# Scheduling the small matmuls of HGRN at top priority in a hybrid encoder trunk

## The chip, the cores and the metric

The kernel runs on one core of a Trainium2 chip. The metric is the device time of one execution in microseconds (us). The engines are named as in the profile: PE is the matmul engine (TensorE) and PEld its loading of weights, DVE the vector engine, ACT the scalar engine, POOL is GpSimd, and SP starts the transfers.

## The reference

The kernel computes a bidirectional encoder trunk: 2 layers, a sequence of 1024 positions, width 1024, float32. Every layer normalises its input, sends it through one projection with 8192 output columns, and lets three groups of heads work on slices of the result side by side: an mLSTM group (4 heads), an HGRN2 group (6 heads of 128 channels) and a differential attention group (4 heads). Each group's output is gated, and one output projection adds the sum to the layer's input. The change touches HGRN only:

```
def hgrn2_chunkwise(q, f, v):            # S_t = diag(f_t) S_{t-1} + (1 - f_t) i_t^T ; o_t = S_t^T q_t
    ...
    A = cumsum(log f)
    decay[t, s, c] = exp(A[t, c] - A[s, c])  for s <= t
    scores = einsum("bhtc,bhtsc,bhsc->bhts", qb, decay, kb)      # kb = 1 - f
    o = scores @ v + (q * exp(A)) @ S_state
    ...
def hgrn2_bidirectional(q, f_fwd, f_bwd, v):
    fwd = hgrn2_chunkwise(q, f_fwd, v)
    bwd = flip(hgrn2_chunkwise(flip(q), flip(f_bwd), flip(v)))
    return fwd + bwd
```

The score of a pair of positions thus weighs each channel by the product of all forget gates between the two.

## The kernel before, in words

**Stages of a layer.** First come the norm and the transposition of the input, then the xm projection with convolution and gates, then two long parts that overlap: the mLSTM recurrence (lines 575 to 663: 4 heads, 8 chunks of 128 positions in each direction; per step the products num, L633 to L638, and the state products st, L648 and L649; per head the products q, L593, and qk, L602), and HGRN with the rest of the projections. Then follow attention with its own projections (aqk, avz), and the output projection (op, L1066).

**Projections.** `proj_channel` (L295) and `proj_token` (L308) multiply the input by blocks of the weight. Each product is split in three matmuls of the type fp32r (high by high, high by low, low by high), with 512 columns streamed in `proj_channel` (tiles pc_...) and 256 or 384 in `proj_token` (tiles pt_...). Their PSUM tiles come from a pair with the tag pj.

**HGRN of one head** (`hgrn_rest`, L684). The query q and the two sets of gates are projected (hq, hff, hfb). Then the scores are built for the 8 chunks of 128 positions at once, by a hierarchy of levels in place of the sum of logarithms. The diagonal (tile dg, L718) is a product of the summed keys kd with q. Level lv (0 to 6) handles pairs of positions that lie in neighbouring blocks of 2^lv positions. For the levels 0 to 4 ACT copies a mixed set of keys to kt (L736), and 16 matmuls (8 chunks by 2 halves, L742) multiply 64 by 64 blocks over 128 channels. DVE then takes the entries of this level into sd by a masked copy (L723). Level 5 has 32 matmuls of 32 by 32, level 6 has 16 of 64 by 64 (L759 and L761), and both write to the PSUM tile that level 4 began. Between the levels DVE multiplies the keys ks (L780) and queries qp (L781) by the gates of the block, and halves the row of gate products (L785). So the levels of a head form a chain: kt and qp of the level, matmuls, then the update for the next. In the program's names all tiles of the levels are lv, those of the diagonal dg. They come from PSUM tiles of 1024 columns with the tag s2, two of them, which the later steps of the head use too: the transposed keys kst, the state products sb and sf, the output ho and its transposition hyT.

The matmuls of dg and lv take float32 operands and write to one half of the partitions, so the trace gives the tile as 128x64 (128x32 at level 5) and two records per matmul: 32 records for a group of 16 matmuls, 64 for level 5.

**What sets the order.** The kernel is written in program order and a scheduler puts it into one list per engine, beforehand, with a simulated timeline. It keeps an order of priority: an instruction's priority is its place in the program, and of those that are ready for an engine the earliest in the program goes first. A PSUM or SBUF slot is given to a tile when its first writer is scheduled. On the chip each engine works through its list. HGRN stands behind mLSTM in the program, and its heads are called in this order:

```
for step in "i0 r0 i1 r1 i2 r2 i3 r3 i4 r4 i5 o0 r5 z0 o1 z1".split():
    {"i": hgrn_iz, "r": hgrn_rest, "o": mlstm_om, "z": mlstm_zm}[step[0]](int(step[1]))
```

Here i is the projection of HGRN's values and gate (hiz, L681), r the rest of a head, o and z are the mLSTM group's gates (om, zm). The tiles qp, ks and T0 of a head have one buffer each, the values v and gates gt two.

Of the kernel before, what the change touches and what calls it, by code (L numbers as in the profile page):

```python
# [17 lines left out]
P = 128  # L18
D = 1024
S = 1024  # L20
NT = S // P
# [64 lines left out]
def raw(ap, off, dims):  # L86
    return bass.AP(ap.tensor, ap.offset + off, [list(ap.ap[0])] + [list(d) for d in dims])
# [3 lines left out]
def trunk(ctx, tc, x_in, positions, w_in, w_out, pvec, rvec, out, dbg=None):  # L91
    nc = tc.nc
# [10 lines left out]
    def ps_mx(name):  # L103
        return pp.tile([P, 512], F32, tag="mx", name=name)

    def ps_s2(name):
        return pp.tile([P, 1024], F32, tag="s2", name=name)
# [239 lines left out]
    for l in range(DEPTH):  # L347
# [14 lines left out]
        for half in range(2):  # L362
# [21 lines left out]
            for k in range(8):  # L384
                ps = ps_mx(f"hT{l}{half}{k}")
# [15 lines left out]
        with tc.tile_pool(name=f"ma{l}", bufs=2) as ma:  # L401
# [38 lines left out]
            for i in range(3):  # L440
                parts = load_win(l, ("xm", i)) if l or i else xm0
                for jj in range(2):
# [19 lines left out]
                    for src, rhs, dd, nm in ((xc, WA[j], xct_d, "a"), (xm, BV[j], v_d, "v")):  # L462
                        tk = ma.tile([P, NT, P], F32, tag="tk", name=f"tk{nm}{l}{j}", bufs=1)
                        for t0 in range(0, NT, 4):
                            ps = ps_s2(f"tk{nm}{l}{j}{t0}")
                            for t in range(4):
                                o = (t // 2) * 512 + (t % 2) * 144
# [27 lines left out]
        with tc.tile_pool(name=f"mb{l}", bufs=1) as mB:  # L495
# [27 lines left out]
            for d in range(2):  # L523
                rows = []
                for nm, src in (("i", igt), ("f", lgf)):
                    rt = mB.tile([4, S], F32, tag="gr" + nm, name=f"gr{nm}{l}{d}", bufs=2)
                    for half in range(2):
                        ps = ps_mx(f"gr{nm}{l}{d}{half}")
# [12 lines left out]
                for c in order:  # L541
                    sl = slice(c * P, (c + 1) * P)
# [10 lines left out]
                for i, (src, dst) in enumerate(((ir, a_tok), (br, b_tok), (mu, m_tok))):  # L553
                    ps = ps_mx(f"gt{l}{d}{i}")
# [17 lines left out]
        with tc.tile_pool(name=f"mc{l}", bufs=1) as mp:  # L572
            for hd in range(MH):
# [14 lines left out]
                q = mp.tile([P, 2, S], F32, tag="m8", name=f"q{l}{hd}", bufs=2)  # L588
                for i, g in enumerate((G[jA], G[jC][:, hh_])):
                    for half in range(2):  # L590
                        sl = slice(half * 512, (half + 1) * 512)
                        ps = ps_mx(f"q{l}{hd}{i}{half}")
# [3 lines left out]
                for half in range(2):  # L596
                    ps = ps_mx(f"qk{l}{hd}{half}")
                    for c4 in range(4):
                        c = half * 4 + c4
                        sl = slice(c * P, (c + 1) * P)  # L600
# [26 lines left out]
                for i in range(NT):  # L627
                    for d in range(2):
                        c = i if d == 0 else NT - 1 - i
                        C = Cs[d]  # L630
                        sl = slice(c * P, (c + 1) * P)
# [11 lines left out]
                        if i < NT - 1:  # L643
                            ks = kst[2 * d + i % 2]
# [22 lines left out]
        def slab(name, tag, bufs=None):  # L667
            return gp.tile([P, S], F32, tag=tag, name=f"{name}{l}", bufs=bufs or 1)
# [15 lines left out]
        def hgrn_rest(hd):  # L684
            v, gt = hvg[hd]
            T0 = gp.tile([P, 2, S], F32, tag="T0", name=f"T0_{l}{hd}")
            qp = gp.tile([P, 2, S], F32, tag="qp", name=f"qp_{l}{hd}")
            ks = gp.tile([P, 2, S], F32, tag="ks", name=f"ks_{l}{hd}")
            q = qp[:, 1]
# [20 lines left out]
            kd = slab(f"kd{hd}", "ha")  # L710
# [1 line left out]
            nc.vector.tensor_tensor(qp[:, 0], T0[:, 0], q, op=ALU.mult)  # L712
            sd = gp.tile([P, NT * 64], F32, tag="sc", name=f"sd{l}{hd}")
            ps = ps_s2(f"dg{l}{hd}")[:, :512]
            for c in range(NT):
                for g in range(2):
                    sl = slice(c * P + g * 64, c * P + g * 64 + 64)
                    nc.tensor.matmul(ps[g * 64:g * 64 + 64, c * 64:c * 64 + 64], kd[:, sl], q[:, sl], start=True, stop=True)  # L718
            nc.scalar.activation(sd, ps, AF.Copy)
            nc.vector.tensor_tensor(qp[:, 1], T0[:, 1], q, op=ALU.mult)  # L720

            def merge(ps, b):
                nc.vector.copy_predicated(sd.rearrange("p (c t) -> p c t", c=NT),  # L723
                                          lvl[b].unsqueeze(1).broadcast_to([P, NT, 64]),
                                          ps[:, :512].rearrange("p (c t) -> p c t", c=NT))
# [4 lines left out]
            pbase = None  # L730
            for lv in range(7):
                hs = 1 << lv
                if lv <= 4:
                    kt = slab(f"kt{hd}{lv}", "kt")
                    nb = S // (2 * hs)
                    nc.scalar.activation(raw(kt, 0, [[2 * hs, nb], [hs, 2], [1, hs]]),  # L736
                                         raw(ks, 0, [[2 * hs, nb], [hs + S, 2], [1, hs]]), AF.Copy)
                    ps = ps_s2(f"lv{l}{hd}{lv}")
                    for c in range(NT):
                        for g in range(2):  # L740
                            o = c * P + g * 64
                            nc.tensor.matmul(ps[g * 64:g * 64 + 64, c * 64:c * 64 + 64], kt[:, o:o + 64],  # L742
                                             raw(qp, o, [[2 * hs, 64 // (2 * hs)], [hs + S, 2], [1, hs]]),
                                             start=True, stop=True)
                    if lv < 4:
                        merge(ps, lv)
                    else:
                        pbase = ps
                else:
                    for c in range(NT):  # L750
                        for m in range(P // (2 * hs)):
                            f0 = 2 * hs * m
                            s0 = f0 + hs
                            b0 = c * P
                            if lv == 5:
                                o1, o2 = c * 64 + hs, c * 64
                            else:
                                o1 = o2 = 512 + c * 64
                            nc.tensor.matmul(pbase[f0:f0 + hs, o1:o1 + hs], ks[:, 0, b0 + f0:b0 + f0 + hs],  # L759
                                             qp[:, 1, b0 + s0:b0 + s0 + hs], start=True, stop=True, skip_group_check=True)  # L760
                            nc.tensor.matmul(pbase[s0:s0 + hs, o2:o2 + hs], ks[:, 1, b0 + s0:b0 + s0 + hs],  # L761
                                             qp[:, 0, b0 + f0:b0 + f0 + hs], start=True, stop=True, skip_group_check=True)
                    if lv == 5:
                        merge(pbase, 4)
                    else:
                        sc = slab(f"sc{hd}", "kt")
                        scv = sc.rearrange("p (c g t) -> p c g t", c=NT, g=2)
                        p6 = pbase[:, 512:].rearrange("p (c t) -> p c t", c=NT)
                        sdv = sd.rearrange("p (c t) -> p c t", c=NT)
                        for g in range(2):  # L770
                            gs = slice(g * 64, g * 64 + 64)
                            nc.scalar.activation(scv[gs, :, 1 - g], p6[gs], AF.Copy)
                            nc.vector.tensor_copy(scv[gs, :, g], sdv[gs])
                nb = S // (2 * hs)
                el = [[2 * hs, nb], [hs + S, 2], [1, hs]]
                tq = raw(T, 1, [[2, nb], [W - 1, 2], [0, hs]])
                tk = raw(T, W + 1, [[2, nb], [-W - 1, 2], [0, hs]])
                qv = raw(qp, 0, el)
                kv = raw(ks, 0, el)
                nc.vector.tensor_tensor(kv, kv, tk, op=ALU.mult)  # L780
                nc.vector.tensor_tensor(qv, qv, tq, op=ALU.mult)  # L781
                base = T1 if lv % 2 == 0 else T0
                a0 = raw(T, 0, [[W, 2], [2, W // 2]])
                a1 = raw(T, 1, [[W, 2], [2, W // 2]])
                nc.vector.tensor_tensor(raw(base, 0, [[W // 2, 2], [1, W // 2]]), a0, a1, op=ALU.mult)  # L785
                T = base
                W //= 2
# [4 lines left out]
            for w in (1, 0):  # L792
                ps = ps_s2(f"kst{l}{hd}{w}")
                for c in range(NT):
                    sl = slice(c * P, (c + 1) * P)
# [4 lines left out]
            for c in range(NT - 1, 0, -1):  # L800
                sl = slice(c * P, (c + 1) * P)
                nc.tensor.matmul(psb[:, sl], kst_t[:, 1, sl], v[:, c], start=True, stop=True)
            for c in range(NT - 1, 0, -1):
                sl = slice(c * P, (c + 1) * P)
# [6 lines left out]
            for c in range(NT - 1):  # L811
                sl = slice(c * P, (c + 1) * P)
                nc.tensor.matmul(psf[:, sl], kst_t[:, 0, sl], v[:, c], start=True, stop=True)
            Sf = ks[:, 0].rearrange("p (c v) -> p c v", c=NT)
            for c in range(NT - 1):
                sl = slice(c * P, (c + 1) * P)
# [7 lines left out]
            for c in range(NT):  # L824
                sl = slice(c * P, (c + 1) * P)
# [6 lines left out]
            for c in range(NT):  # L832
                sl = slice(c * P, (c + 1) * P)
                nc.scalar.activation(jk, po[:, sl], AF.Square, accum_out=ss[:, c:c + 1])
            rstd(ss, r, P)
            for c in range(NT):
                sl = slice(c * P, (c + 1) * P)
                nc.vector.scalar_tensor_tensor(gt[:, c], po[:, sl], r[:, c:c + 1], gt[:, c], op0=ALU.mult, op1=ALU.mult)
            ps = ps_s2(f"hyT{l}{hd}")
            for c in range(NT):  # L840
                sl = slice(c * P, (c + 1) * P)
# [59 lines left out]
        for step in "i0 r0 i1 r1 i2 r2 i3 r3 i4 r4 i5 o0 r5 z0 o1 z1".split():  # L901
            {"i": hgrn_iz, "r": hgrn_rest, "o": mlstm_om, "z": mlstm_zm}[step[0]](int(step[1]))
# [3 lines left out]
        with tc.tile_pool(name=f"at{l}", bufs=2) as ap, tc.tile_pool(name=f"aw{l}", bufs=1) as aw:  # L906
# [79 lines left out]
            for hd in range(AH):  # L986
# [5 lines left out]
                for qt in range(NT):  # L992
                    qs = slice(qt * P, (qt + 1) * P)
                    ex, ls = [], []
                    for n in range(2):
                        ps = ps_s2(f"S{l}{hd}{qt}{n}")
# [20 lines left out]
                    for kb in range(2):  # L1017
                        ps = ps_mx(f"wT{l}{hd}{qt}{kb}")
# [28 lines left out]
        for jp in (3, 4, 5, 0, 1, 2, 6, 7):  # L1047
# [3 lines left out]
            for j in range(2):  # L1051
                for half in range(2):
                    sl = slice(half * 512, (half + 1) * 512)
# [4 lines left out]
            for tt in range(NT):  # L1058
                ts = slice(tt * P, (tt + 1) * P)
                for nb in range(2):  # L1060
                    ps = (ps_pj if nb == 0 or jp in OP_PJ else ps_mx)(f"op{l}{jp}{tt}{nb}")
# [14 lines left out]
    with tc.tile_pool(name="fin", bufs=3) as fp_:  # L1076
        fg = fp_.tile([P, D], F32, name="fg", bufs=1)
        nc.sync.dma_start(fg, rvec[DEPTH * RVN:DEPTH * RVN + D].partition_broadcast(P))
        for tt in range(NT):
# [7 lines left out]
            o = fp_.tile([P, D], F32, tag="o", name=f"fo{tt}")  # L1087
# [77 lines left out]
```

## Time and profile before

| | us |
|---|---|
| median of 3 runs | 2874.41 (2874.36 to 2874.71) |
| the profiled execution | 2875.73 |
| its span | 2873.9 |
| layer 0, HGRN from its first diagonal product to the attention projections | 211 to 912 |
| layer 1, the same | 1636 to 2335 |

The profile is one execution, recorded instruction by instruction. The span runs from its first instruction to its last. Busy time is summed over the instructions of an engine; for PE the ends of matmuls are modelled, because they are pipelined, while the starts are recorded. That is why durations of neighbouring matmuls overlap in the timeline, and why the distance from one start to the next is what a matmul takes. A row of the timeline is a stretch of like instructions: start, time from the first start to the last end, engine, line, operation, tiles written and read, tile of the array, shape of the streamed operand, count.

### The profile page before, as it was taken

What the parts mean: (1) busy time and instruction counts of PE and PEld (TensorE: products, weight loads), DVE (VectorE), ACT (ScalarE), POOL (GpSimd) and SP (SyncE); (2) the same over time, 40 slices, a digit from 0 to 9 for tenths busy, and PEclk for the clock granted to TensorE, in tenths of its full rate; (3) what the DMA queues carried; (4) which work ended last, traced back from release to release, by engine and by line L of the source; (5) the groups of instructions that cost most, each with busy time, mean ns of one, the idle gap of its engine ahead of it and who ended that gap; (6) DMA issues with size and microseconds to landing.
All of it is one profiled execution on the core that took longest, in us unless ns stands there. A gap on an engine that the chain in (4) does not pass through costs nothing.

```text
span 2873.9 us, 49824 instructions
## 1 busy us (share of the span) xinstructions
PE 2781.5 (97%) x19876; PEld 2470.0 (86%) x19876; DVE 1865.2 (65%) x4054; ACT 1078.3 (38%) x2454; POOL 633.3 (22%) x554
## 2 busy tenths in 40 slices
PE   6999999999999999999999999999899999999998
PEld 5888888888888999888879788888798989998886
DVE  6667767576464576796565577676565636767865
ACT  4333433323333445542243333332233325545423
POOL 2122323212123111012211323132122231111112
PEclk9999999999999999999999999999999999999999
DMA  3422212211122111222324221221111221103132
GB/s 120 128 75 68 93 53 74 82 56 45 44 97 96 30 30 38 91 71 91 115 82 132 90 63 54 73 93 46 44 45 58 85 94 30 38 30 118 59 94 100
DMA packets 129863, 210.18 MB, mean 73 GB/s; under 512 B 10832, under 2 KB 60496, under 8 KB 129632
## 3 DMA queue, kind: packets, MB, share of 16 engines
q1 hardware_dynamic: 129632, 207.01, 22.1%
q8 instruction: 156, 2.56, 0.4%
q14 instruction: 75, 0.61, 0.1%
HBM read 156.58 MB, written 50.40 MB: 72 GB/s over the span
## 4 chain that ended last, share of the span: by engine, by line
PE 81%; DVE 8%; issue 6%; DMA 2%; ACT 2%; POOL 1%; SPq 0%; DVEq 0%; ACTq 0%; POOLq 0%
PE op L1066 11%; PE pt_hiz L308 7%; PE pt_aqk L308 6%; PE pt_avz L308 6%; PE pc_zm L295 5%; PE pc_hff L295 5%; PE pc_hq L295 4%; PE pc_hfb L295 4%; PE pc_xm L295 4%; PE po L1027 3%; PE lv L742 2%; PE pt_om L308 2%; PE S L1000 2%; PE S L999 2%; PE wT L1020 2%
## 5 line engine op out<-in xcount | busy, mean ns | idle before, releaser
L137 POOL TENSOR_TENSOR wlo<-wraw,whi 128x512 fp32r<-128x512 f32 x320 | 441.2, 1401 | 1602.1 <-ACT whi L136 1536.5
L1066 PE MATMUL op<-whi,yb 128*128 128x512 f32 x1024 | 334.4, 399 | 1.1 <-DVE yb L1057 0.5
L136 ACT ACTIVATE whi<-wraw 128x512 fp32r<-128x512 f32 x320 | 184.4, 625 | 302.9 <-PE op L1066 82.2
L1070 DVE TENSOR_TENSOR xo<-op,xo 128x512 f32<-128x512 f32 x256 | 175.1, 688 | 99.7 <-PE op L1066 99.5
L1066 PEld LDWEIGHTS op<-whi,yb 128*128 128x128 f32 x1024 | 192.6, 188 | 46.4 <-DVE yb L1057 1.4
L308 PE MATMUL pt_hiz<-whi,hh 128*128 128x256 f32 x768 | 225.4, 294 | 2.6 <-DVE hg L680 2.5
L308 PE MATMUL pt_hiz<-whi,hl 128*128 128x256 f32 x768 | 224.4, 292 | 0.0
L308 PE MATMUL pt_hiz<-wlo,hh 128*128 128x256 f32 x768 | 223.2, 291 | 0.0
L1066 PE MATMUL op<-wlo,yb 128*128 128x512 f32 x512 | 201.9, 394 | 0.0
L1006 ACT ACTIVATE e<-S,mx 128x1024 f32<-128x1024 f32 x128 | 142.3, 1113 | 124.8 <-DVE mx L1003 106.2
L645 POOL TENSOR_SCALAR ks<-xcth,wsv 128x192 f32<-128x192 f32 x112 | 108.1, 967 | 289.3 <-PE st L649 271.1
L1002 DVE TENSOR_REDUCE mx<-S 128x1 f32<-128x1024 f32 x128 | 155.0, 1218 | 12.7 <-PE S L1000 12.0
L308 PEld LDWEIGHTS pt_hiz<-whi,hh 128*128 128x128 f32 x768 | 146.6, 191 | 7.1 <-DVE hg L680 3.5
L308 PE MATMUL pt_avz<-whi,hh 128*128 128x256 f32 x512 | 145.9, 285 | 4.4 <-DVE ag L962 4.4
L308 PEld LDWEIGHTS pt_hiz<-whi,hl 128*128 128x128 f32 x768 | 146.7, 191 | 2.3 <-issue 1.0
L308 PEld LDWEIGHTS pt_hiz<-wlo,hh 128*128 128x128 f32 x768 | 146.6, 191 | 1.7 <-issue 0.5
L308 PE MATMUL pt_aqk<-whi,hh 128*128 128x256 f32 x512 | 146.1, 285 | 0.0
L308 PE MATMUL pt_avz<-whi,hl 128*128 128x256 f32 x512 | 145.5, 284 | 0.0
L308 PE MATMUL pt_avz<-wlo,hh 128*128 128x256 f32 x512 | 145.2, 284 | 0.0
L308 PE MATMUL pt_aqk<-whi,hl 128*128 128x256 f32 x512 | 145.2, 284 | 0.0
L308 PE MATMUL pt_aqk<-wlo,hh 128*128 128x256 f32 x512 | 144.8, 283 | 0.0
L1027 PE MATMUL po<-av,wT 128*128 128x128 f32 x1024 | 135.3, 275 | 4.8 <-DVE mx L1003 3.5
(359 smaller groups left out, 7563.2 us busy)
## 6 DMA issues: line engine op xcount, KB each, us to landing
wraw<-w_in SPq DMA_DIRECT2D x256, 256.0 KB, 2.8
wraw<-w_out SPq DMA_DIRECT2D x64, 256.0 KB, 2.7
yr<-yT SPq DMA_DIRECT2D x64, 256.0 KB, 3.0
xac<-xcd SPq DMA_DIRECT2D x16, 512.0 KB, 7.1
W<-mu SPq DMA_DIRECT2D x32, 256.0 KB, 3.6
xcd<-xc SPq DMA_DIRECT2D x12, 512.0 KB, 3.0
xct<-tka SPq DMA_DIRECT2D x12, 512.0 KB, 3.2
vd<-tkv SPq DMA_DIRECT2D x12, 512.0 KB, 3.2
```

The costliest lines, as they stand in the source:

```text
L136: nc.scalar.activation(hi[:, o:o + m], rw[:, :m], AF.Copy)
L137: nc.gpsimd.tensor_sub(lo[:, o:o + m], rw[:, :m], hi[:, o:o + m].bitcast(F32))
L295: nc.tensor.matmul(ps, a[:, c0:c0 + P], b[:, k], start=(i == 0), stop=(i == 23))
L308: nc.tensor.matmul(ps[:, :n], a[:, k, ts], b, start=(i == 0), stop=(i == 23))
L645: nc.gpsimd.tensor_scalar(ks[:, k0:k0 + MD], xct[:, c], wsv[:, d, c, hd:hd + 1], None, op0=ALU.mult)
L742: nc.tensor.matmul(ps[g * 64:g * 64 + 64, c * 64:c * 64 + 64], kt[:, o:o + 64], raw(qp, o, [[2 * hs, 64 // (2 * hs)], [hs + S, 2], [1, hs] ...
L999: nc.tensor.matmul(ps[:, kb_s], Q1[:, n, qs], KH[:, n, kb_s], start=True, stop=False)
L1002: nc.vector.tensor_reduce(mx, ps, axis=AX.X, op=ALU.max)
L1006: nc.scalar.activation(e, ps, AF.Exp, scale=QK ** -0.5, bias=mx, accum_out=ls_)
L1027: nc.tensor.matmul(po[:, :P], wT[:, t * P:(t + 1) * P], v[:, t], start=(t == 0), stop=(t == NT - 1))
L1066: nc.tensor.matmul(ps, a[:, j, ts], b[:, cs_], start=(i == 0), stop=(i == 5))
L1070: nc.vector.tensor_tensor(xv, ps, xv, op=ALU.add)
```

## The change

The matmuls of the diagonal and of the levels are put into a block `tc.high_priority()`. The guard sets the priority of what is traced inside it to that of the start of the program, and restores it at the end of the block. Nothing else differs: the same instructions, operands, tiles and dependencies. The loops inside are only indented.

```diff
             ps = ps_s2(f"dg{l}{hd}")[:, :512]
-            for c in range(NT):
-                for g in range(2):
-                    sl = slice(c * P + g * 64, c * P + g * 64 + 64)
-                    nc.tensor.matmul(ps[g * 64:g * 64 + 64, c * 64:c * 64 + 64], kd[:, sl], q[:, sl], start=True, stop=True)
+            with tc.high_priority():
+                for c in range(NT):
+                    for g in range(2):
+                        sl = slice(c * P + g * 64, c * P + g * 64 + 64)
+                        nc.tensor.matmul(ps[g * 64:g * 64 + 64, c * 64:c * 64 + 64], kd[:, sl], q[:, sl], start=True, stop=True)
...
                     ps = ps_s2(f"lv{l}{hd}{lv}")
-                    for c in range(NT):
-                        for g in range(2):
+                    with tc.high_priority():
+                        for c in range(NT):
+                            for g in range(2):
...
                 else:
-                    for c in range(NT):
-                        for m in range(P // (2 * hs)):
+                    with tc.high_priority():
+                        for c in range(NT):
+                            for m in range(P // (2 * hs)):
...
```

More of the change, by code (lines that the diff above doesn't have):

```diff
@@ L738, in hgrn_rest @@
                     ps = ps_s2(f"lv{l}{hd}{lv}")
-                    for c in range(NT):
-                        for g in range(2):
[L741 to L744, printed above, removed]
+                    with tc.high_priority():
+                        for c in range(NT):
+                            for g in range(2):
+                                o = c * P + g * 64
+                                nc.tensor.matmul(ps[g * 64:g * 64 + 64, c * 64:c * 64 + 64], kt[:, o:o + 64],
+                                                 raw(qp, o, [[2 * hs, 64 // (2 * hs)], [hs + S, 2], [1, hs]]),
+                                                 start=True, stop=True)
                     if lv < 4:
@@ L749, in hgrn_rest @@
                 else:
-                    for c in range(NT):
-                        for m in range(P // (2 * hs)):
[L752 to L762, printed above, removed]
+                    with tc.high_priority():
+                        for c in range(NT):
+                            for m in range(P // (2 * hs)):
+                                f0 = 2 * hs * m
+                                s0 = f0 + hs
+                                b0 = c * P
+                                if lv == 5:
+                                    o1, o2 = c * 64 + hs, c * 64
+                                else:
+                                    o1 = o2 = 512 + c * 64
+                                nc.tensor.matmul(pbase[f0:f0 + hs, o1:o1 + hs], ks[:, 0, b0 + f0:b0 + f0 + hs],
+                                                 qp[:, 1, b0 + s0:b0 + s0 + hs], start=True, stop=True, skip_group_check=True)
+                                nc.tensor.matmul(pbase[s0:s0 + hs, o2:o2 + hs], ks[:, 1, b0 + s0:b0 + s0 + hs],
+                                                 qp[:, 0, b0 + f0:b0 + f0 + hs], start=True, stop=True, skip_group_check=True)
                     if lv == 5:
```

## The prediction

> **What bounds the kernel now.** I began with the first lines of the page: the span, and the busy time, share and instructions of each engine.
>
> ```profile
> span 2873.9 us, 49824 instructions
> ## 1 busy us (share of the span) xinstructions
> PE 2781.5 (97%) x19876; PEld 2470.0 (86%) x19876; DVE 1865.2 (65%) x4054; ACT 1078.3 (38%) x2454; POOL 633.3 (22%) x554
> ```
>
> PE is busy in 97% of the span, the next engine, DVE, in 65%. A busy PE need not be a productive one, so the question for this change is how many of PE's microseconds are lost between matmuls of different kinds. HGRN runs from about 211 to 912 us in layer 0 and from 1636 to 2335 us in layer 1. The table by stage splits each of these where the mLSTM recurrence ends beside it (layer 0) or is near its end (layer 1); the columns are the stretch, its length, then busy time and instruction count of each engine.
>
> ```profile
> 211.00:632.00 421.00, 409.83 (x3380) 361.70 (x3380) 295.13 (x758) 139.34 (x347) 118.04 (x133) 0.99 0.22 72
> 632.00:912.00 280.00, 276.08 (x2053) 244.34 (x2050) 153.71 (x292) 92.60 (x233) 67.22 (x43) 1.00 0.21 69
> ...
> 1636.00:1950.00 314.00, 306.87 (x2509) 268.07 (x2508) 219.61 (x567) 108.46 (x275) 93.91 (x109) 1.00 0.25 79
> 1950.00:2335.00 385.00, 376.45 (x2891) 335.69 (x2889) 225.53 (x454) 122.96 (x304) 87.39 (x60) 0.99 0.20 65
> ```
>
> PE (first busy column) leaves 11.2, 3.9, 7.1 and 8.6 us idle in the four stretches, 30.8 us together, at a granted clock of 0.99 to 1.00; DVE is busy for 70% of the first and the third. In these stretches PE is the bound: what shortens its queue shortens the stretch, as long as other ready work stands behind it. The waits of PE show how rarely it lacks work. These are its waits between 2040 and 2060 us, where layer 1 has no mLSTM work left to run in between (total us, times, longest):
>
> ```profile
> PE lv L759 <- DVE qp L781: 3.1, 1, 3.1
> PE kst L796 <- DVE ks L780: 1.3, 1, 1.3
> ```
>
> This is its one long wait between 448 and 455 us, where a num stands inside a diagonal group:
>
> ```profile
> PE num L633 <- issue: 2.7, 1, 2.7
> ```
>
> And this is all that the matmuls of the level groups (first line) and of the diagonal groups (second line) wait for in the whole execution, us and times: 4.0 us together.
>
> ```profile
>   DVE qp L781: 3.2, 2
>   DVE kd L711: 0.8, 3
> ```
>
> **What the change removes.** No instruction, wait or transfer is added or dropped; priorities of 576 matmuls (48 per head, 12 heads, two records each in the trace) go to those of the program's start. So I looked for what stands between the matmuls of one group now. There are 96 groups: diagonal, levels 0 to 4, level 5, level 6, for each of 12 heads; 32 records each, 64 at level 5. This is a cut one in the timeline of PE (start us, duration, operation, count):
>
> ```profile
> 492.22 0.28 PE L308 MATMUL pt_hiz<-whi,hl 128*128 128x256 f32 x1
> 492.43 0.80 PE L742 MATMUL lv<-qp,kt 128*64 128x64 f32 x18
> 493.16 0.59 PE L633 MATMUL num<-vth,W 128*128 128x193 f32 x2
> 493.59 0.49 PE L637 MATMUL num<-C,q 128*128 128x193 f32 x2
> 493.92 0.49 PE L638 MATMUL num<-C,q 128*128 128x193 f32 x2
> 494.34 0.56 PE L742 MATMUL lv<-qp,kt 128*64 128x64 f32 x10
> 494.83 0.59 PE L648 MATMUL st<-vth,ks 128*128 128x193 f32 x2
> 495.26 0.49 PE L649 MATMUL st<-vth,ks 128*128 128x193 f32 x2
> 495.68 0.34 PE L742 MATMUL lv<-qp,kt 128*64 128x64 f32 x4
> 495.95 0.39 PE L308 MATMUL pt_hiz<-whi,hh 128*128 128x256 f32 x1
> 496.17 0.28 PE L308 MATMUL pt_hiz<-wlo,hh 128*128 128x256 f32 x1
> ```
>
> The group of 32 lies in three pieces, 18, 10 and 4, with ten mLSTM records in the two cuts. And this is a whole one:
>
> ```profile
> 617.12 0.28 PE L308 MATMUL pt_hiz<-whi,hl 128*128 128x256 f32 x1
> 617.33 1.15 PE L742 MATMUL lv<-qp,kt 128*64 128x64 f32 x32
> 618.41 0.39 PE L308 MATMUL pt_hiz<-whi,hh 128*128 128x256 f32 x1
> ```
>
> From the group's first start to the next projection's start the cut one takes 495.95 - 492.43 = 3.52 us, the whole one 618.41 - 617.33 = 1.08 us. The difference, 2.44 us, holds the ten foreign records and what the two cuts cost. What the foreign records cost where they stand among projections is in this piece of the timeline:
>
> ```profile
> 499.17 0.28 PE L308 MATMUL pt_hiz<-whi,hh 128*128 128x256 f32 x1
> 499.29 0.49 PE L648 MATMUL st<-vth,ks 128*128 128x193 f32 x2
> 499.61 0.49 PE L649 MATMUL st<-vth,ks 128*128 128x193 f32 x2
> 499.80 0.41 PE L308 MATMUL pt_hiz<-wlo,hh 128*128 128x256 f32 x1
> 500.06 0.28 PE L308 MATMUL pt_hiz<-whi,hl 128*128 128x256 f32 x1
> 500.18 0.28 PE L308 MATMUL pt_hiz<-whi,hh 128*128 128x256 f32 x1
> ```
>
> From 499.17 to 500.18 run three projection records and four st records. Projections start 0.12 us apart (500.06 to 500.18), so the four st take 1.01 - 0.36 = 0.65 us, 0.163 each, which is the pace at which they follow one another (499.29 to 499.61 for two). Between full-width matmuls there is thus no price for a change of kind. Ten foreign records are worth 1.63 us, and the two cuts in the small group cost 2.44 - 1.63 = 0.81 us, **0.40 us a cut**. In the rows: the first lv record comes 0.21 us after the projection before it instead of 0.12, the first num 0.43 us before the next pair instead of 0.33, and again on the way back.
>
> I walked through all records of L718, L742, L759 and L761 in the same way: 41 of the 96 groups are cut, by 62 cuts (30 in layer 0, 32 in layer 1). The first and the last of the cuts have these rows behind them:
>
> ```profile
> 222.01 0.37 PE L742 MATMUL lv<-qp,kt 128*64 128x64 f32 x2
> ...
> 1951.91 0.27 PE L761 MATMUL lv<-qp,ks 128*64 128x64 f32 x1
> ```
>
> What stands in the cuts is 394 records of mLSTM work (num, st, q, qk and one pair of gt transposes), all of it earlier in the program than the group it cuts; no projection ever cuts one. So the order follows program position, and a group with the position of the program's start can be cut by nothing that is ready. Group length less the median length of a whole group of that level, less the foreign records at their own pace, gives 30.5 us for the 62 cuts; six of them, in five groups, also hold waits or a slow group start (8.8 us). The other 56 cost 21.7 us, 0.39 each, with groups between 0.33 and 0.51 a cut.
>
> **The sum.** 62 cuts by 0.39 us = 24.2 us of PE's queue. On the path: all of it, since PE is the bound in both stretches and the mLSTM matmuls land next to a group or among projections. There they cost nothing extra: a full-width matmul behind a small group pays what the projection pays that stands there now (the num at 493.16 holds up its second pair by 0.10 us, 0.43 for 0.33; the projection at 495.95 its follower by 0.10 us, 0.22 for 0.12). Full groups keep their own entry and exit. Where a group is brought forward, the DVE and ACT steps that read it come up to 2.44 us earlier; these engines have room, so I cost that at nothing. Where mLSTM work is put behind a group, it waits for the rest of the group: summed over the 41 groups, by the share of the records still to run, 26 us over both layers. That cover is the projections of the same stretch: PE does them meanwhile. What is late next is still PE. SP's and POOL's queues keep their order as far as the priorities go, and the PSUM slots (two of the kind that the groups use) are asked for within a head one after the other, so the earlier claim passes no other claimant that I can name.
>
> Ends for the 24.2: the low one is 62 x 0.33 = 20.5 us; the high one is 30.5 us, if the waits in the six odd cuts go too. The new order shifts everything behind the first cut, and what such a shift is worth by itself I take from the two layers, which run the same program in different orders. From an early xm matmul to the first aqk matmul of each layer the table by stage has
>
> ```profile
> 37.84:912.12 874.28, 855.09 (x6448) 753.62 (x6447) 557.51 (x1278) 291.56 (x706) 217.90 (x202) 0.99 0.23 74
> 1455.25:2335.07 879.82, 857.03 (x6447) 755.28 (x6447) 554.53 (x1215) 288.12 (x699) 217.36 (x201) 0.99 0.23 73
> ```
>
> 874.3 and 879.8 us: 5.5 us apart. So -24.2 with ends of -36 and -15 (30.5 + 5.5 and 20.5 - 5.5). The profiled execution took 2875.73 us, 1.8 above its span, and stands 1.3 us above the median of 2874.41; the sum is a difference and carries over: 2874.4 - 24.2 = **2850.2 us**.
>
> The Trainium skill, "TensorEngine Tiling (Array Packing)", section Tiling Modes, says that a change of the tiling mode drains the array, and "TensorE: Matmul & The Clock Gate", Single matmul latency, puts that drain near 175 ns; two changes a cut would be 0.35 us and the sum 21.7 us, an estimate by those pages. The rows' 0.39 us is what I use.
>
> **The rivals.** (1) *PE runs dry.* Inside a head the levels are a serial chain through DVE, and the projections of the next head that may run beside it are limited. Where no mLSTM work is left, PE already waits (the 3.1 us for qp and 1.3 us for ks near 2050 us). If PE gets through its queue earlier and then waits for the chain in half of the places, half of the gain is left: -12, 2862 us. Against it: the idle time in these stretches is 30.8 of 1400 us, 2.2%, now, and each cut that goes also shortens the chain.
>
> (2) *It does not do what it says.* If the matmuls of a group become ready one by one, or another claim on slots cuts them, the cuts stay: 2874 us. Against it: 55 groups run whole today.
>
> (3) *Slower: PE held at the head of a group.* In the trace the num that waited 2.7 us (row above) held up the rest of the diagonal group behind it: PE doesn't pass a matmul that waits. A group now goes ahead of mLSTM work that is ready; if on the chip its qp or kt comes later than the scheduler thought, all of PE stands still. One level step of DVE is the size of such a delay:
>
> ```profile
> L780 DVE TENSOR_TENSOR ks<-ks,T x84: 1187/1218/3280, 212.1 to 2267.1; 128x1024 f32<-128x1024 f32 x84
> ```
>
> At 1.2 us for each of the 41 groups that is 49 us, less 24 gained: +25, 2899 us. It decides from 0.6 us a group on. Against it: today a group's first matmul is as exposed as it will be, and the groups wait 4.0 us in all. The Trainium skill, "TensorE: Matmul & The Clock Gate", section Packing small matmuls, has matmuls start in strict program order; by that rule this rival is real wherever an input is late, and the trace agrees with its 2.7 us.
>
> **How the numbers follow.** The forecast gets 0.62, rival 1 0.18, rival 2 0.10, rival 3 0.10. A measurement of this kernel can tell about 0.2% (5.7 us) from no change, so faster means below 2868.7 us: the forecast's case and nearly all of rival 1, 0.79; within 0.2% 0.11; slower 0.10. The forecast's own range is 2838 to 2859; with rival 1 the range that holds 8 in 10 is 2837 to 2869.
>
> **What would show it.** In the changed profile every diagonal and level group is one row of x32 (at levels 5 and 6 an unbroken run of 64 and 32) in PE's timeline, about 1.08 us to the next start; PE's idle time in the two HGRN stretches stays near 31 us; the two stretches from xm to aqk become about 12 us shorter each (862 and 867 us); the attention and output stages keep their lengths. Wrong: groups still cut (rival 2); whole groups but PE's waits on qp, kt, n or C grown by 10 us or more (rivals 1 and 3); or mLSTM matmuls dearer at their new places than 0.163 us a record.

## The result, and the profile after

The changed kernel takes 2826.86 us (median of 4 runs, 2825.65 to 2828.33), the kernel before 2874.56 us beside it (2874.36 to 2875.56): a ratio of 0.9831, 95% interval 0.9819 to 0.9842. It is faster by 47.7 us. The forecast was a gain of 24.2 us, and the low end of its wider range 2837 us. So the gain was twice what was forecast, and the time lies below the range.

The first lines of the page after:

```profile
span 2826.6 us, 49802 instructions
## 1 busy us (share of the span) xinstructions
PE 2748.2 (97%) x19876; PEld 2457.4 (87%) x19876; DVE 1868.1 (66%) x4054; ACT 1080.6 (38%) x2454; POOL 648.9 (23%) x554
```

PE has the same 19876 records and is busy for 33.3 us less (2781.5 before). The span has shrunk by 47.3, so 14 us of PE's idle time went as well. All of it lies in the HGRN stage. In the table by stage, from the first diagonal matmul to the first aqk matmul of each layer (stretch, length, busy time and count of PE, PEld, DVE, ACT, POOL, granted clock, share of the DMA engines, GB/s), the kernel before has

```profile
211.80:911.90 700.10, 685.01 (x5417) 605.28 (x5417) 448.05 (x1050) 231.74 (x578) 184.46 (x176) 1.00 0.22 71
1636.60:2334.90 698.30, 682.62 (x5393) 603.29 (x5393) 445.14 (x1021) 231.34 (x578) 181.19 (x169) 0.99 0.22 71
```

and the changed kernel

```profile
211.80:888.10 676.30, 668.01 (x5418) 599.68 (x5417) 453.95 (x1050) 232.09 (x578) 192.51 (x176) 1.00 0.23 73
1612.40:2286.90 674.50, 667.62 (x5394) 598.07 (x5393) 442.25 (x1021) 233.19 (x579) 189.51 (x170) 1.00 0.23 74
```

Both stretches are 23.8 us shorter, 47.6 together. PE's idle time in them (length less busy) falls from 15.1 and 15.7 us to 8.3 and 6.9: 30.8 to 15.2. The other 32 us are busy time for the same work. PE's waits in the stages fall at two places: at HGRN's own matmuls (dg, lv and those of the head's end, and the gate projection hff, which waits for ACT to write qp) from 12.7 to 2.5 us, and at mLSTM's matmuls (num, st, q, qk, gt) from 14.1 to 9.5 us.

All 96 groups are whole now, and 0 cuts are left. This is a group with mLSTM work at hand, in PE's timeline after (the level matmuls are L744 now):

```profile
1851.58 0.28 PE L308 MATMUL pt_hiz<-whi,hl 128*128 128x256 f32 x1
1851.79 1.22 PE L744 MATMUL lv<-qp,kt 128*64 128x64 f32 x32
1852.94 0.59 PE L648 MATMUL st<-vth,ks 128*128 128x193 f32 x2
1853.38 0.49 PE L649 MATMUL st<-vth,ks 128*128 128x193 f32 x2
1853.57 0.41 PE L308 MATMUL pt_hiz<-whi,hh 128*128 128x256 f32 x1
1853.82 0.28 PE L308 MATMUL pt_hiz<-wlo,hh 128*128 128x256 f32 x1
1853.94 0.49 PE L633 MATMUL num<-vth,W 128*128 128x193 f32 x2
```

The st that would have cut the group stands right behind its 32 records, and the num comes two projection records later. The projection behind the st starts 0.19 us after the start of the st's last row, as it does among projections.

The chain of levels has become shorter. In head 2 of layer 0 it runs from the first diagonal record at 448.79 us to the end of the last level-6 record at 514.68 us before, and from 434.86 to 475.85 us after. Added up over the twelve heads this is 657 us before and 534 us after. Of these 123 us, 120 went in heads 0 to 3, which run beside mLSTM or its end.

PE's granted clock is the third thing that changed. The kernel before had four spells at half clock near or in these stretches (the clock is the third number from the right, 0.50):

```profile
329.80:333.20 3.40, 3.40 (x15) 3.40 (x14) 3.33 (x10) 0.94 (x3) 0.54 (x2) 0.50 0.23 81
452.70:456.10 3.40, 3.40 (x22) 2.88 (x22) 2.89 (x5) 0.93 (x2) 0.00 (x0) 0.50 0.02 5
1630.30:1637.10 6.80, 6.80 (x43) 6.56 (x44) 3.23 (x5) 2.92 (x6) 2.44 (x8) 0.50 0.58 154
2053.60:2060.40 6.80, 5.48 (x46) 5.29 (x43) 3.01 (x5) 2.68 (x4) 0.00 (x0) 0.50 0.01 2
```

Two of them begin beside waits of PE that the prediction quoted (2.7 us until 452.4, 3.1 us until 2053.2). The changed kernel has one such spell:

```profile
1617.70:1621.10 3.40, 3.40 (x6) 1.34 (x6) 3.40 (x6) 0.93 (x4) 0.00 (x0) 0.50 1.10 340
```

Within the stages that is 14.2 us at half clock before (of the spell at 1630 only the last 0.5 us lies inside) and 3.4 after. At half speed a microsecond does half a microsecond's work, so this is worth some 5 us, an estimate. What is left of the 47.6 us, after 15.6 of waits and 5 of clock, is 27 us for the 62 cuts, 0.43 each, where the prediction had 0.39.

### The profile page after: what moved, and what is told of

The parts are those of the page before. It is cut to its first block, busy times and chain, and to the rows that moved or that the text cites. A ratio compares the mean times of both kernels' runs of the same rounds, so it can differ in the third digit from the quotient of the medians.

```text
span 2826.6 us, 49802 instructions
## 1 busy us (share of the span) xinstructions
PE 2748.2 (97%) x19876; PEld 2457.4 (87%) x19876; DVE 1868.1 (66%) x4054; ACT 1080.6 (38%) x2454; POOL 648.9 (23%) x554
## 4 chain that ended last, share of the span: by engine, by line
PE 79%; DVE 5%; issue 2%; DMA 2%; ACT 2%; POOL 0%; DVEq 0%; SPq 0%; ACTq 0%; POOLq 0%
PE op L1069 12%; PE pt_aqk L308 6%; PE pt_avz L308 6%; PE pt_hiz L308 6%; PE pt_om L308 5%; PE pc_zm L295 5%; PE pc_hq L295 4%; PE pc_hff L295 4%; PE po L1030 4%; PE pc_hfb L295 3%; PE lv L744 2%; PE pc_xm L295 2%; PE wT L1023 2%; PE S L1003 2%; PE S L1002 2%
## 5 line engine op out<-in xcount | busy, mean ns | idle before, releaser
L645 POOL TENSOR_SCALAR ks<-xcth,wsv 128x192 f32<-128x192 f32 x112 | 122.2, 1093 | 313.4 <-PE st L649 267.7
```

The costliest lines, as they stand in the source:

```text
L645: nc.gpsimd.tensor_scalar(ks[:, k0:k0 + MD], xct[:, c], wsv[:, d, c, hd:hd + 1], None, op0=ALU.mult)
```

## The experiments

Five theories were on trial. A: a cut costs 0.39 us, and the rest of the gain came from waits of PE and the clock. B: the whole gain is the price of the cuts, 0.77 us each. C: the waits went by the luck of another order. D: mLSTM work, put behind the groups, lasts longer and covers the end of HGRN's head 3. E, which came later: mLSTM work inside a group holds up the group's end, so that the serial chain of levels is longer and PE lacks work. For each run stand PE's cuts, idle time and half clock in the two HGRN stages together, taken as above; kernels that were run together had the same chip and the same runs of the kernel before beside them.

**The price of a cut.** Two twins do the same added work, once in the middle of the group and once behind it:

```diff
+            # x1: inside, after the 8th of 16 matmuls (diagonal; likewise for levels 0 to 3)
+                    if c == 3:
+                        nc.tensor.matmul(pd[:, 512:640], kd[:, :P], q[:, :P], start=True, stop=True)
+            # x2: the same line behind the loop over c
```

> The changed kernel with one extra full-width float32 product (128 columns, result unread) after the eighth of the 16 matmuls in each of 60 groups (diagonal and levels 0 to 3): it cuts each of them once. Against the twin that has the same 60 products behind the groups, theory A (a cut costs 0.39 us, the rest of the gain came from fewer waits and the clock) expects +23 us (60 x 0.39), theory B (the whole gain of 47.7 us came from the 62 cuts, 0.77 us each) expects +46 us. In numbers: A 2863 us, B 2886 us.

> The changed kernel with the same 60 extra full-width products, each behind its group, so that no group is cut. Both theories expect the price of the products alone: 60 x 2 records x 0.112 us = 13 us over the changed kernel, 2840 us.

The first took 2861.2 us (ratio to before 0.9949, 0.9934 to 0.9964), the second 2840.0 (0.9874, 0.9857 to 0.9890). The products alone cost 13.2 us over the changed kernel, as expected of both theories. Their place inside costs 21.2 us, 0.35 for each of 60 cuts: A's 23, not B's 46. A cut group of the first in PE's timeline:

```profile
669.67 0.28 PE L308 MATMUL pt_hiz<-whi,hh 128*128 128x256 f32 x1
669.88 0.89 PE L747 MATMUL lv<-qp,kt 128*64 128x64 f32 x16
670.70 0.49 PE L751 MATMUL lv<-qp,kt 128*128 128x128 f32 x2
671.12 0.89 PE L747 MATMUL lv<-qp,kt 128*64 128x64 f32 x16
671.93 0.39 PE L308 MATMUL pt_hiz<-wlo,hh 128*128 128x256 f32 x1
```

and the like group of the second:

```profile
666.31 1.56 PE L746 MATMUL lv<-qp,kt 128*64 128x64 f32 x32 [0.17 <-DVE qp L723]
667.79 0.49 PE L750 MATMUL lv<-qp,kt 128*128 128x128 f32 x2
668.04 0.36 PE L308 MATMUL pt_hiz<-whi,hl 128*128 128x256 f32 x1
```

From the group's start to the next projection: 2.05 us against 1.73, 0.32 for the cut. PE's idle time is 12.0 and 15.4 us, so 60 cuts by so short a product bring no waits with them. B's price of 0.77 us is refuted.

**Order or luck.** Two changes of order that have nothing to do with the groups, each with and without the priority:

```diff
-                    for d in range(2):                                  # x4, x5: mLSTM step
+                    for d in (1, 0):
...
-            proj_channel(parts, P, h, mkf(0), f"hff{l}{hd}")            # x6, x7: HGRN's gates
-            proj_channel(load_win(l, ("hfb", hd)), 0, h, mkf(1), f"hfb{l}{hd}")
+            pb = load_win(l, ("hfb", hd))
+            proj_channel(pb, 0, h, mkf(1), f"hfb{l}{hd}")
+            proj_channel(parts, P, h, mkf(0), f"hff{l}{hd}")
```

> The kernel before with the two directions of each mLSTM step in the other program order, a change of order that has nothing to do with the groups; 63 cuts in the list of PE. All theories: near the kernel before, 2868 to 2881 us. Its use is the pair with the same swap and priority.

> The changed kernel with the same swap; no cuts. Theory A by pace: 40 to 50 us below its pair, since cuts, waits and half clock go together. Theory C (waits went by luck): 25 us below its pair (63 x 0.39), give or take 8 for the luck of the two orders. Theory B: 63 x 0.77 = 48 us below.

> The kernel before with the backward gate of HGRN projected ahead of the forward gate, a second change of order that has nothing to do with the groups; 56 or 57 cuts. All theories: 2866 to 2881 us.

> The changed kernel with the same exchange of the gates; no cuts. Theory A by pace: 38 to 48 us below its pair. Theory C: 22 us below (56 x 0.39), give or take 8. Theory B: 43 us below.

| kernel | us | ratio to before (95%) | cuts | PE idle | half clock |
|---|---|---|---|---|---|
| before | 2874.6 | | 62 | 30.8 | 14.2 |
| changed | 2826.9 | 0.9831 (0.9819 to 0.9842) | 0 | 15.2 | 3.4 |
| x4 swapped, before | 2874.0 | 0.9993 (0.9984 to 1.0002) | 63 | 29.2 | 14.0 |
| x5 swapped, changed | 2826.1 | 0.9829 (0.9812 to 0.9847) | 0 | 14.7 | 0.0 |
| x6 gates, before | 2865.2 | 0.9967 (0.9954 to 0.9980) | 56 | 26.6 | 10.9 |
| x7 gates, changed | 2827.0 | 0.9828 (0.9813 to 0.9843) | 0 | 8.4 | 4.6 |

The pairs differ by 47.7, 47.9 and 38.2 us. In every one the waits fall by 14 to 18 us, and the three kernels with whole groups lie within 1 us of one another. C is refuted for the bulk of the waits: they go together with the cuts in all three pairs, and the half clock falls with them. An order alone can move the time, too: x6 lies 9.7 us below the kernel before that ran beside it, just below the 2866 us that were the least expected.

**What makes the waits go.** Priority for the chain in place of the matmuls, and priority for a part of the groups:

```diff
+            with tc.high_priority():      # x3, on the kernel before: around each DVE and ACT step of the levels
+                nc.scalar.activation(sd, ps, AF.Copy)
...
-            with tc.high_priority():      # x8: only around the matmuls of levels 0 to 4
```

> The kernel before, with top priority for the DVE and ACT steps of the levels (copies to kt, merges, products of ks, qp and T) in place of the matmuls. The list of PE has 64 cuts as against 62. If the waits and the half clock went because HGRN's heads now run faster beside mLSTM (theory A, by pace), they go here too, while the cuts stay: about 24 us less than before, 2850 us. If they went by the luck of another order (theory C), no more than some 6 us either way: 2868 to 2880 us. Theory B (cuts alone): 2874 us.

> Top priority for the matmuls of levels 0 to 4 alone; the list of PE keeps 29 cuts (diagonal and levels 5 and 6). Theory A by pace: 29 x 0.39 = 11 us above the changed kernel, 2838 us, most waits gone. Theory B: 29 x 0.77 = 22 us above, 2849 us. Theory C: anywhere from 2838 to 2862 us, as the waits fall.

x3 took 2885.7 us (1.0034, 1.0021 to 1.0047): slower than before by 10 us, above what A, B and C expected. It is a miss for A's idea that HGRN's pace only needs priority for these steps, but no test of what a faster chain does: added up over the twelve heads, as above, the chains take 678 us, more than the 657 before. It has 65 cuts in its trace, 41.0 us of idle time and 13.7 at half clock. Most of what was added are waits of mLSTM's q matmuls on their transfer and on ACT (7.8 and 4.2 us over both layers, as against 1.6 and 1.9 before). Why these grew stays open. x8 took 2851.7 us (0.9916, 0.9901 to 0.9930) with 29 cuts, 23.8 us idle and 6.8 at half clock: between the two kernels in all three, and so are its chains (582 us). It is 25 us above the changed kernel, where A had 11 and B 22; most waits had not gone, as A expected them to. The cuts at 0.39 us are 11 of the 25, the idle time 9 and the half clock some 2.

Then theory D, by moving or leaving out the last mLSTM steps:

```diff
-                for i in range(NT):                                    # y2, on the changed kernel
+                for i in range(NT if hd < 3 else 4):
...
+                        # y1 (on the kernel before) and y3 (on the changed one): around the whole step
+                        with (tc.high_priority(offset=-2880) if hd == 3 and i >= 4 else nullcontext()):
```

> The kernel before, without any priority for the groups; the second half of the last mLSTM head's steps (4 of 8 steps, all engines) gets a lower priority, behind HGRN's head 3, so that it runs beside that head's end. 57 cuts stay of 62. Theory D (a part of the gain came because mLSTM work, put behind the groups, lasted longer and covered the end of HGRN's head 3): PE's waits after the last mLSTM product fall from 12.5 us to 3 or less, and the half clock near the end of head 3 in layer 1 (6.8 us, worth 3.4) goes, with 2 us from the 5 cuts: about 15 us below before, 2860 us. Theory C (those waits went by the luck of the order): no fall of these waits, 2868 to 2880 us.

> The changed kernel that leaves out steps 4 to 7 of the last mLSTM head in both directions and both layers: 72 records of 0.163 us a layer, 23.5 us of PE's work. Theory D: with mLSTM at its end earlier, the end of HGRN's head 3 is bare again, 10 us of waits and 3 to 5 us of half clock come back: 2815 to 2818 us. Without such a cover the work is simply gone: 2803 us.

> The changed kernel with the same late half of the last mLSTM head. Theory D: the end of head 3 is covered already (1.5 us of waits after the last mLSTM product), so little is left to gain: 2821 to 2829 us. A further fall of 10 us or more would say that the cover is worth more than theory D has it.

y1 took 2868.6 us (0.9974, 0.9964 to 0.9985). The edit moved the end of mLSTM by 8 and 30 us only, and the waits after it fell from 12.5 to 8.4 us, not to the 3 that D expected, with 28.7 us idle in all. The time is 9 us above D's 2860 us, but the cover was hardly longer in layer 0: no clear test. y2 took 2806.7 us (0.9754, 0.9735 to 0.9773), 20 us below the changed kernel, where 23.5 us of work were left out and D expected 9 to 12. Waits after mLSTM's end rose from 1.5 to 5.7 us, PE's idle time from 15.2 to 17.5. y3 took 2829.6 us (0.9834, 0.9813 to 0.9856): the cover was longer by 45 us in each layer and nothing was gained, the time being 0.6 us above D's range. So D holds for some 4 us and not for the bulk.

E was tried from two sides, by work in the middle of groups that is as long as the mLSTM work in the kernel before, and by a longer chain without any work for PE:

```diff
+                    if c == 3 and hd < 4:                                # z1; z2 has it behind the loop
+                        for _ in range(2):
+                            nc.tensor.matmul(pd[:, 512:], kd[:, :P], q[:, :512], start=True, stop=True)
...
+                    for _ in range(3 if hd < 4 else 1):                  # z3
                         nc.scalar.activation(raw(kt, 0, [[2 * hs, nb], [hs, 2], [1, hs]]),
```

> The changed kernel with two extra full-width float32 products of 512 columns (4 records, 1.72 us, results unread) in the middle of the diagonal and of levels 0 to 3 of heads 0 to 3: 40 groups cut once each, their ends held up by 2.1 us, much like the 41 cut groups of the kernel before. Against the twin with the same products behind the groups: the cuts alone give 40 x 0.40 = +16 us. Theory E (a group held up makes the chain of levels longer, and PE waits and drops its clock for it): another 10 to 20 us, +26 to +36 in all, and PE's idle time in the two stages 10 us or more above the twin's. Luck of the order: +16 +- 6, idle alike.

> The same 80 products, each pair behind its group. Work alone: 40 x 4 x 0.429 = 69 us over the changed kernel, 2896 us, under all theories.

> The changed kernel with the copy to kt made three times over in levels 0 to 4 of heads 0 to 3 (ACT, 1.04 us each, the same data): no cut, no work for PE, but the matmuls of 40 groups become ready up to 2.1 us later (less where DVE's product for qp is later still). Theory E: PE's waits and half clock come back in good part, +10 to +20 us over the changed kernel. Otherwise within 5 us of it.

> The changed kernel once more, beside the other three on the same chip: 2827 us, idle 15 us in the two stages under all theories.

z2 took 2892.2 us (1.0059, 1.0044 to 1.0074), z1 2904.5 (1.0102, 1.0087 to 1.0117): 12.4 us apart, 0.31 a cut, with idle times of 7.2 and 6.5 us. E expected 26 or more, so this is a miss for E as it was stated. But both twins have 67 us more work for PE in the same stages, and their idle time is half that of the changed kernel: with so much to do PE does not run out of work, and the twins cannot show waits.

z3 adds nothing to PE. It took 2847.4 us (0.9909, 0.9892 to 0.9926), the changed kernel beside it 2825.3 (0.9828, 0.9813 to 0.9842): +22.1 us, a little more than the 10 to 20 us that E expected. Its stages have

```profile
212.00:895.70 683.70, 670.59 (x5417) 599.24 (x5417) 451.13 (x1050) 273.15 (x619) 193.47 (x176) 1.00 0.23 72
1619.30:2304.30 685.00, 669.17 (x5394) 597.67 (x5394) 441.26 (x1021) 271.60 (x619) 188.56 (x170) 1.00 0.22 73
```

against these of the changed kernel that ran beside it:

```profile
212.00:886.90 674.90, 667.75 (x5418) 599.79 (x5418) 453.10 (x1050) 231.44 (x578) 193.19 (x177) 1.00 0.23 73
1613.40:2287.30 673.90, 668.03 (x5394) 598.29 (x5394) 442.24 (x1021) 232.82 (x578) 187.95 (x170) 1.00 0.23 74
```

PE is idle for 28.9 us as against 13.0, nearly the 30.8 of the kernel before, with no cut at all. The half clock did not come back, though E expected it: z3 has none in its stages, z4 has 3.8 us. The chains of the twelve heads, as above, take 614 us as against 532 in z4. At the end of the stage in layer 1 three of the kernel before's four longest waits are back, without the 3.1 us for qp. From the end of mLSTM in layer 1 to the end of the stage, PE's longest waits (total us, times, longest) are in the kernel before

```profile
PE lv L759 <- DVE qp L781: 3.1, 1, 3.1
PE ho L826 <- DVE Sb L808: 1.7, 1, 1.7
PE kst L796 <- DVE ks L780: 1.3, 1, 1.3
PE pc_hff L295 <- ACT qp L693: 0.9, 1, 0.9
```

in z3

```profile
PE ho L830 <- DVE Sb L812: 1.7, 1, 1.7
PE kst L800 <- DVE ks L784: 1.3, 1, 1.3
PE pc_hff L295 <- ACT qp L693: 0.9, 1, 0.9
```

and in the changed kernel none over 0.5 us:

```profile
PE pc_zm L295 <- DVE zg L892: 0.5, 1, 0.5
PE pt_hiz L308 <- DVE hg L680: 0.2, 1, 0.2
PE dg L719 <- DVE kd L711: 0.2, 1, 0.2
```

Over both stages z3 has 18.3 us of waits at HGRN's matmuls, where z4 has 2.1, and 6.5 at mLSTM's, where z4 has 7.0. So a longer chain brings back waits of the first kind alone, more of them than the 12.7 us of the kernel before; that the sum of both comes near to 30.8 is chance. One doubt stays: z3 also gives ACT 83 us more work, and 5.3 us of its waits are gate projections that wait for ACT (3.3 in the kernel before, none in z4). Without them 13.0 us are left, still far above z4's 2.1.

**A faster kernel?** Two steps beyond the change: priority for the full-width products of each head's end too, and the masked copy of a level moved behind the products for the next level; then both.

```diff
+                with tc.high_priority():          # y4: kst; likewise sb, sf, ho
                     for c in range(NT):
...
-                    if lv < 4:                    # w1; w2 is y4 and w1 together
-                        merge(ps, lv)
...
                 W //= 2
+                if lv < 4:
+                    merge(ps, lv)
+                elif lv == 5:
+                    merge(pbase, 4)
```

> The changed kernel with top priority for the full-width products of the end of each HGRN head too (transposed keys, state products, output). These are full width, so no cuts are saved. Theory A: 0 +- 6 us against the changed kernel, 2821 to 2833 us. If priority itself helped by HGRN's pace, 10 us or more below it, under 2817 us.

> The changed kernel with the masked copy of levels 0 to 3 and 5 (0.74 us on DVE) behind the products for the next level in program order, so that it is off the chain of levels: up to 5 x 0.74 = 3.7 us less chain per head, 44 us over the 12 heads. Theory E (the chain's length sets the waits): waits fall further, by up to the 8 us of the two stages that are not mLSTM's own, 2817 to 2823 us. If the chain is no bound any more: 2824 to 2830 us.

> The same, with top priority for the products of each head's end as well (that alone gave 2822 us). Theory E: 2813 to 2819 us. If the chain is no bound: as with the priority alone, 2820 to 2825 us.

y4 took 2822.3 us (0.9811, 0.9790 to 0.9832), w1 2823.3 (0.9819, 0.9806 to 0.9832), w2 2826.3 (0.9833, 0.9819 to 0.9846). All are faster than the kernel before; against the changed kernel's 0.9831 and 0.9828 the intervals overlap, so none is shown to be faster than it. In w1 PE's idle time is 13.9 us, of which 10.6 are waits of mLSTM's own matmuls and 0.7 waits of HGRN's. The time falls between E's range and the other one, and w2 above both. With whole groups the chain of levels is no longer what PE waits for, and to shorten it further gains nothing that can be told.

## Why the prediction was right and wrong

**Right: the cuts.** All 62 went, mLSTM work stands behind the groups and costs there what it costs among projections. The price of 0.39 us a cut held roughly: 0.35 and 0.31 in the twins, 0.43 if all that is left over in the accounting is put on the cuts. The term of 24.2 us is then 19 to 22 by the twins and 27 at most. The count of matmuls beside it is wrong, but no term rests on it: the trace has 3456 records of dg and lv, so 1728 matmuls, 144 per head, and not 576.

**Right: mLSTM can wait.** The 26 us by which its steps were expected to be put off were costed at nothing. It now ends 18 and 46 us later within its stages, more than those 26, and PE's waits at its matmuls have not grown for it (14.1 us before, 9.5 after).

**Wrong: "the DVE and ACT steps that read it come up to 2.44 us earlier; these engines have room, so I cost that at nothing".** That was the step that failed. These steps are links of a serial chain, and whether DVE has room does not matter to a chain. In 41 of the 96 groups the chain was longer by the mLSTM work and the cut, 2.44 us in the quoted case, some 90 us over 41 groups (65 us of foreign records and the cuts). In the trace the chains are 123 us shorter in all. PE's idle time, which the prediction expected to stay near 31 us, fell to 15.2, and the spells at half clock went from 14.2 to 3.4 us. Together that is some 21 us of gain that the sum had at zero, most of what lies between 24 and 47.7. z3 shows the step by itself: the chain made longer in 40 groups, without a cut, brings 16 us of waits back and costs 22 us. That accounts for the 10 us of waits that went at HGRN's matmuls. The 4.6 us at mLSTM's are not shown to be the chain's (2.7 of the waits there were the one of num inside a diagonal group), nor are the 5 us of the clock: two of the three whole spells that went, at 329.8 and 452.7 us, began behind waits of num.

**Rival 1 had the mechanism with the wrong sign.** It named the chain through DVE and even the waits near 2050 us, but as something that would eat the gain. That "each cut that goes also shortens the chain" stood there as an argument against the rival and was not carried into the sum. The 30.8 us of idle time in the four stretches were at hand as a term that could shrink; the high end of -36 took in only the waits inside the cut groups (5.5 us of PE's idle time) and the 5.5 us between the layers.

**The other rivals.** The change did what it says, so rival 2 fell. Rival 3 fell: the waits of the groups' own matmuls are 2.4 us in the changed kernel (4.0 before).

**Open.** 15.6 us of waits, 5 of clock and 19 to 22 of cuts make 40 to 43 us of the 47.7. The other 5 to 8 are not settled. z3 has some us of the same kind: in the profiled executions, which are 17.0 us apart, its stages are 19.9 us longer than z4's, 15.9 idle and 4.0 busy for the same work, without a cut and without half clock. So such time may go with the waits; that is argued, not shown. How much of the waits is owed to the chain and how much to the longer cover (4 us in y2) was not told apart to better than that, and z1, in which E failed, leaves E shown by z3 alone, beside the lengths of the chains.

## What to carry to other kernels

When matmuls are put in another order, two sums are due: what PE saves by itself, and by how much the chain that reads these matmuls becomes shorter, set against the idle time of PE in the same stage. A busy share of 97% does not settle the second: a good part of the idle 2% can be the chain's, here 10 of the 15.6 us that went. A group of narrow matmuls that feeds a serial chain belongs together and ahead of work that can wait, and a twin with the same work behind the group instead of inside it prices a cut without a theory.

## What the runs showed of the hardware that was not expected

Into and out of a group of 128x64 matmuls PE pays, and between full-width matmuls of float32 and fp32r it does not: 0.31 to 0.43 us a cut against 0.163 us a record for mLSTM products anywhere among projections. The prediction's estimate from the Trainium skill, "TensorEngine Tiling (Array Packing)", section Tiling Modes, with the drain that the Trainium skill gives in "TensorE: Matmul & The Clock Gate", Single matmul latency, was 0.35 us; the twins' 0.35 and 0.31 agree with it.

Some short waits cost twice. In the kernel before a wait of 1.7 us that ended at 328.8 us (a num for DVE) was followed at 329.8 by 3.4 us at half clock, and one of 3.1 us by 6.8. The Trainium skill, "TensorE: Matmul & The Clock Gate", Part 1, has the clock fall after an idle window of about 3.4 us. The lengths of the spells in this trace, 3.4 us and twice that, agree with such a window. The waits ahead of them were shorter than it (1.7, 2.7 and 3.1 us), and others of 1.5 us had no spell behind them, nor had those of z3's stages, up to 2.6 us. The spells do not begin at any time: those at 329.82, 452.70 and 2053.55 us lie 36 and 469 steps of 3.413 us apart. So what a wait of this size costs in clock may depend on where it falls between such steps; no run here was made to tell.
